# Fifteen small loads between two bulk loads of a row-maximum kernel

## The chip, the cores and the metric

The kernel runs on one core of a Trainium2 chip. The metric is the device time of one execution in microseconds (us). The core's engines that matter here are VectorE (DVE in the profile), which reduces, SyncE (SP), which issues the DMAs that load the input, and the core's 16 DMA engines, which move the bytes.

## The reference

```python
def setup_inputs():
    rows = 8192
    cols = 8192
    return {"x": np.random.randn(rows, cols).astype(np.float32)}

def reference(x):
    return np.linalg.norm(x, ord=np.inf, axis=1)
```

With an axis given, the infinity norm is that of each row as a vector: the largest absolute value of each of the 8192 rows. The input has 268 MB, the output 32 KB.

## The kernel before

The rows are split into two parts. The first 48 rows of each of the 128 partitions are the bulk, the last 16 the tail.

**The bulk.** Two loops, over `a` (six rounds) and `n` (four steps), issue 24 loads from SP (L263). Each brings two rows of 8192 floats to each partition: a tile of 128 x 16384 floats, 8 MB. The tiles lie in `ring`, which has three slots, used in turn. Behind each load stands one reduction on VectorE (L251, in the helper `absmax`), which writes two maxima per partition into `r_bulk`. From the fourth load on, a load has to wait until the reduction three places earlier has freed its slot.

**The tail.** The last 16 rows of each partition come in 30 loads (L296) of decreasing width, from 13056 floats down to 640, listed in `TAIL`. They lie in the same ring. The reductions of the tail write partial maxima into gaps of the ring, and in the end one maximum per row into `r_tail`. Two stores end the kernel: `r_bulk` from ScalarE's queue (L314), three pieces before the end, and `r_tail` from SP (L316).

**What orders the work.** Every engine works through its own list in order; a DMA waits on its issuing engine, here SP, so what is behind it in SP's list waits too. The framework gives each DMA one of eight completion counters in turn (`DMAHW0` to `DMAHW7`, lanes in what follows), and has a DMA wait until the last one on the same lane has landed. [...] The function `drop_implied_waits` strikes out such a wait where SP's wait for VectorE already implies it: a reduction that is over had waited for its load. In SP's list of the kernel before, the 24 bulk loads have no wait for a lane left, only the wait for the reduction that frees their slot; from the fifteenth load of the tail on, the loads have waits for lanes as well, some of them beside a wait for VectorE. Three further functions move the first load to the head of SP's list, let the Pool engine finish the program, and take VectorE out of the opening barrier.

`ring` has 3 x 16384 + 128 floats per partition and is the last tile that is taken from the pool.

Of the kernel before, what the change touches and what calls it, by code (L numbers as in the profile page):

```python
# [12 lines left out]
F32 = mybir.dt.float32  # L13
# [195 lines left out]
@with_exitstack  # L209
def kernel(  # L210
    ctx: ExitStack,
    tc: tile.TileContext,
    x: bass.AP,
    out: bass.AP,
    G: int = 4,
    B: int = 2,
    SLOTS: int = 3,
    PAD: int = 128,
):
    nc = tc.nc  # L220
    P = nc.NUM_PARTITIONS
    rows, cols = x.shape
    W = B * cols
    R = SLOTS * W + PAD * 4


    n_tail = sum(w for _, w in TAIL) // cols
    met = 0
    for lo, w in sorted(TAIL):
        assert lo == met  # L230
        met += w
    assert met == n_tail * cols
    n_bulk_rows = rows // P - n_tail
    assert n_bulk_rows % (G * B) == 0
    A = n_bulk_rows // (G * B)
    split = n_bulk_rows * P
    x_b = x[:split].rearrange("(a p n b) c -> a n p (b c)", p=P, a=A, n=G, b=B)
    out_b = out[:split].rearrange("(a p n b) -> p a (n b)", p=P, a=A, n=G, b=B)
    x_t = x[split:].rearrange("(p t) c -> p (t c)", p=P)
    out_t = out[split:].rearrange("(p t) -> p t", p=P)  # L240

    pool = ctx.enter_context(tc.tile_pool(name="sbuf", bufs=1))
    r_bulk = pool.tile([P, A, G * B], F32)
    r_tail = pool.tile([P, n_tail], F32)
    used = [HEAD, A * G * B, n_tail]
    gap = -sum(-(-n // STEP) * STEP for n in used) % PAD
    pool.tile([P, gap], F32, name="gap")
    ring = pool.tile([P, R], F32)

    def absmax(o, i):  # L250
        return nc.vector.reduce_max(  # L251
            out=o, in_=i, axis=X, apply_absolute_value=True
        )

    def after(ins, first, kind):
        info = mybir.DependencyInfo(kind, mybir.DependencyReason.SCHED_ONLY)
        tc.add_manual_dep(ins.ins, first.ins.name, info, reason="order")

    for a in range(A):
        for n in range(G):  # L260
            at = (a * G + n) % SLOTS * W
            t = ring[:, at : at + W]
            nc.sync.dma_start(out=t, in_=x_b[a, n])  # L263
            absmax(
                r_bulk[:, a, n * B : (n + 1) * B],
                t.rearrange("p (b c) -> p b c", b=B),
            )


    pieces = []  # L270
    for j, (at, w) in enumerate(TAIL):
        end = at + w
        while at < end:
            r = at // cols
            to = min(end, (r + 1) * cols)
            pieces.append((j, r, to - at))
            at = to
    of_row = [[k for k, s in enumerate(pieces) if s[1] == r] for r in range(n_tail)]


    here = A * G % SLOTS * W
    start, slot = [], []
    for j, (_, w) in enumerate(TAIL):
        first = next(s for s in pieces if s[0] == j)
        ks = of_row[first[1]]
        n_part = len(ks) - 1 if pieces[ks[-1]][0] == j else 0
        at = -(-(here + n_part) // PAD) * PAD
        if at + w > R:
            at = -(-n_part // PAD) * PAD
        start.append(at)  # L290
        slot.append(at - n_part)
        here = at + w

    for j, (src, w) in enumerate(TAIL):
        at = start[j]
        nc.sync.dma_start(out=ring[:, at : at + w], in_=x_t[:, src : src + w])  # L296
        here = [k for k, s in enumerate(pieces) if s[0] == j]
        offs = [at + sum(pieces[i][2] for i in here[:m]) for m in range(len(here))]
        todo = list(zip(here, offs))
        if slot[j] != at:  # L300

            todo = todo[1:] + todo[:1]
        for k, lo in todo:
            _, r, n = pieces[k]
            ks = of_row[r]
            if k == ks[-1]:
                frm = slot[j] if len(ks) > 1 else lo
                done = absmax(r_tail[:, r : r + 1], ring[:, frm : lo + n])
            else:
                to = slot[pieces[ks[-1]][0]] + ks.index(k)  # L310
                done = absmax(ring[:, to : to + 1], ring[:, lo : lo + n])
        if j == len(TAIL) - 3:

            ins = nc.scalar.dma_start(out=out_b, in_=r_bulk[:])  # L314
            after(ins, done, mybir.DependencyClass.Sync)
    nc.sync.dma_start(out=out_t, in_=r_tail[:])  # L316
    nc.at_finalize(drop_implied_waits)
    nc.at_finalize(start_first_load_early)
    nc.at_finalize(finish_on_pool)
    nc.at_finalize(open_without_vector)  # L320
# [30 lines left out]
```

## Time and profile before

| What | Value |
|---|---|
| Median of 2 runs | 626.54 us (626.53 to 626.56) |
| The profiled execution's own time | 626.59 us |
| Its span, first to last instruction | 624.0 us |
| VectorE busy | 552.5 us, 66 reductions |
| Read from HBM | 268.44 MB, 430 GB/s over the span with what is written |
| One bulk reduction | 17.22 us |
| VectorE idle before the bulk reductions | 70.5 us in all, the longest 22.0 us |
| SP waiting for VectorE ahead of bulk loads | 417.1 us in 21 waits |
| A bulk load, issue to landing, median | 40.7 us |

A profile's span is shorter than the time of the execution by what lies before its first and behind its last instruction. In the tables of waits, the engine that waits stands on the left, and what ended its wait on the right; "SPq" is SP's list of DMAs. A DMA "lands" when its counter has its last count. The time from issue to landing includes the time in which the DMA lies in the queue behind earlier ones.

### The profile page before, as it was taken

To read this page: it belongs to the slowest core of one execution; us is meant where nothing else is said; L and a number is where in the kernel's file an instruction comes from. 1 tells how busy PE (TensorE), PEld (TensorE's weight loads), DVE (VectorE), ACT (ScalarE), POOL (GpSimd) and SP (SyncE) were. 2 spreads that over 40 slices of the span, in tenths; PEclk is the share of its full clock that TensorE was granted. 3 is DMA by queue.
4 is the path that set the end of the run, shared out by engine and by line. 5 is a ranking of instruction groups with operands and counts; after the bars stand their busy time and mean duration, and the time that the engine had idled before them with its cause. 6 is when DMAs were issued, how large, how long until landed. Compare 5 with 4: busy or idle time off the path is not lost.

```text
span 624.0 us, 153 instructions
## 1 busy us (share of the span) xinstructions
DVE 552.5 (89%) x66; POOL 0.2 (0%) x4
## 2 busy tenths in 40 slices
DVE  0588988889988899888898888988889999999999
POOL 0000000000000000000000000000000000000000
DMA  9999999999999999999999999999999999999998
GB/s 403 458 416 450 424 441 433 403 471 403 471 403 458 416 454 420 450 424 420 454 403 471 403 466 408 458 416 454 420 436 432 417 446 420 428 433 429 429 426 345
DMA packets 8561, 268.47 MB, mean 430 GB/s; under 512 B 1648, under 2 KB 1648, under 8 KB 3184
## 3 DMA queue, kind: packets, MB, share of 16 engines
q1 hardware_dynamic: 7776, 268.44, 99.6%
q10 hardware_dynamic: 784, 0.02, 0.1%
q14 instruction: 1, 0.01, 0.0%
HBM read 268.44 MB, written 0.03 MB: 430 GB/s over the span
## 4 chain that ended last, share of the span: by engine, by line
DMA 64%; DVE 35%; another core or an unknown queue 0%; issue 0%; DVEq 0%; SPq 0%
DMA ring<-in_x_dram 64%; DVE r_bulk L251 25%; DVE r_tail L251 7%; DVE ring L251 3%; DVEq L346 0%; SPq L296 0%
## 5 line engine op out<-in xcount | busy, mean ns | idle before, releaser
L251 DVE TENSOR_REDUCE r_bulk<-ring 128x2 f32<-128x16384 f32 x24 | 413.3, 17220 | 70.5 <-DMA ring<-in_x_dram 70.5
L251 DVE TENSOR_REDUCE ring<-ring 128x1 f32<-128x4736 f32 (+20 forms) x26 | 70.5, 2759 | 0.2 <-DMA ring<-in_x_dram 0.2
L251 DVE TENSOR_REDUCE r_tail<-ring 128x1 f32<-128x8192 f32 (+12 forms) x16 | 70.5, 4428 | 0.0
L335 POOL MEMSET const-bfloat16-1.0<- 128x1 bf16 x1 | 0.1, 103 | 0.0
L335 POOL MEMSET const-uint8-127<- 128x1 uint8 x1 | 0.1, 102 | 0.0
L335 POOL MEMSET const-float32-1.0<- 128x1 f32 x1 | 0.1, 100 | 0.0
L335 POOL MEMSET const-float32-0.0<- 128x1 f32 x1 | 0.1, 99 | 0.2 <-issue 0.2
## 6 DMA issues: line engine op xcount, KB each, us to landing
ring<-in_x_dram SPq DMA_DIRECT2D x1, 6528.0 KB, 32.7
ring<-in_x_dram SPq DMA_DIRECT2D x1, 6464.0 KB, 36.6
ring<-in_x_dram SPq DMA_DIRECT2D x1, 5824.0 KB, 27.1
ring<-in_x_dram SPq DMA_DIRECT2D x1, 5184.0 KB, 39.0
ring<-in_x_dram SPq DMA_DIRECT2D x1, 4672.0 KB, 36.8
ring<-in_x_dram SPq DMA_DIRECT2D x1, 4096.0 KB, 32.7
ring<-in_x_dram SPq DMA_DIRECT2D x1, 3648.0 KB, 40.9
ring<-in_x_dram SPq DMA_DIRECT2D x1, 3264.0 KB, 36.8
```

Source lines behind the costliest of these rows:

```text
L251: return nc.vector.reduce_max(out=o, in_=i, axis=X, apply_absolute_value=True)
L335: nc = _bacc.Bacc("TRN2", target_bir_lowering=False, num_devices=1)
```

## The change

A further tile `marks` of 16 partitions x 256 floats is taken from the pool behind `ring`. When the loop over the bulk has issued the load of `a == 2`, `n == 1`, the tenth of the 24, SP issues fifteen further loads, for k = 1 to 15. The k-th reads 16 floats (64 bytes) from each of the first k rows of the same block of the input and writes them to k partitions of `marks`, each to columns of its own. Nothing reads `marks`. The eleventh bulk load follows.

```diff
@@ -246,6 +246,7 @@
     gap = -sum(-(-n // STEP) * STEP for n in used) % PAD
     pool.tile([P, gap], F32, name="gap")
     ring = pool.tile([P, R], F32)
+    marks = pool.tile([16, 256], F32)
 
     def absmax(o, i):
         return nc.vector.reduce_max(
@@ -261,6 +262,12 @@
             at = (a * G + n) % SLOTS * W
             t = ring[:, at : at + W]
             nc.sync.dma_start(out=t, in_=x_b[a, n])
+            if a == 2 and n == 1:
+                for k in range(1, 16):
+                    nc.sync.dma_start(
+                        out=marks[:k, 16 * k : 16 * k + 16],
+                        in_=x_b[a, n][:k, 16 * k : 16 * k + 16],
+                    )
             absmax(
                 r_bulk[:, a, n * B : (n + 1) * B],
                 t.rearrange("p (b c) -> p b c", b=B),
```

In SP's list of the changed program the fifteen loads take the lanes 2 to 7, 0 to 7 and 0. The first five have no wait. The sixth to the fifteenth each wait for the lane that they take, and so do the eight bulk loads that follow them, these beside their wait for VectorE. The list of VectorE is the same.

## The prediction

> I number the 24 bulk loads 0 to 23 in the order in which they are issued. The fifteen small loads stand behind load 9 (a = 2, n = 1) and ahead of load 10; I call them s1 to s15 by their partition count.
>
> **What bounds the kernel now.** I read the page first: the two rows of busy tenths, the chain that ended last and the costliest group.
>
> ```profile
> span 624.0 us, 153 instructions
> ...
> DVE 552.5 (89%) x66; POOL 0.2 (0%) x4
> ...
> DMA  9999999999999999999999999999999999999998
> ...
> DMA ring<-in_x_dram 64%; DVE r_bulk L251 25%; DVE r_tail L251 7%; DVE ring L251 3%; DVEq L346 0%; SPq L296 0%
> ...
> L251 DVE TENSOR_REDUCE r_bulk<-ring 128x2 f32<-128x16384 f32 x24 | 413.3, 17220 | 70.5 <-DMA ring<-in_x_dram 70.5
> ```
>
> The DMA row is at 9 in every slice but the last. VectorE is 89% busy, but it idles before each bulk reduction, and what it waits for is the load. So the load stream is the bound, from the first microsecond to the end: a gap in it is paid in full unless later work can catch it up. The chain names VectorE for 35%, yet VectorE and the transfers only alternate there; the stream never stops under it.
>
> Next the timeline around load 9, VectorE and SP's queue in turn:
>
> ```profile
> 22.04 17.22 DVE L251 TENSOR_REDUCE r_bulk<-ring 128x2 f32<-128x16384 f32 x1 [22.04 <-DMA ring<-in_x_dram]
> 41.34 17.22 DVE L251 TENSOR_REDUCE r_bulk<-ring 128x2 f32<-128x16384 f32 x1 [2.08 <-DMA ring<-in_x_dram]
> ...
> 155.27 0.33 SPq L263 DMA_DIRECT2D ring<-in_x_dram  x1
> 157.42 17.22 DVE L251 TENSOR_REDUCE r_bulk<-ring 128x2 f32<-128x16384 f32 x1 [2.18 <-DMA ring<-in_x_dram]
> 174.67 0.33 SPq L263 DMA_DIRECT2D ring<-in_x_dram  x1
> 176.74 17.22 DVE L251 TENSOR_REDUCE r_bulk<-ring 128x2 f32<-128x16384 f32 x1 [2.10 <-DMA ring<-in_x_dram]
> ...
> 196.03 17.22 DVE L251 TENSOR_REDUCE r_bulk<-ring 128x2 f32<-128x16384 f32 x1 [2.07 <-DMA ring<-in_x_dram]
> ...
> 215.34 17.22 DVE L251 TENSOR_REDUCE r_bulk<-ring 128x2 f32<-128x16384 f32 x1 [2.09 <-DMA ring<-in_x_dram]
> ```
>
> The bulk reductions follow each other by load, so the one at 22.04 is load 0's, at 41.34 load 1's, at 157.42 load 7's, at 176.74 load 8's, at 196.03 load 9's and at 215.34 load 10's. A reduction starts 0.02 us after its load has landed. The step from one landing to the next is 19.3 us, and a load that starts into an idle queue (load 0, issued at 0.00) needs 22.02 us: 2.7 us more than its share of a running stream. SP issues load 9 at 155.27 (the end of load 6's reduction, which frees its slot) and load 10 at 174.67 (the end of load 7's). While load 9 is being moved, load 10 has thus been in the queue for 21 us. Nothing else stands in the queue behind load 9 before 174.67.
>
> Last, what SP waits for, what one of its issues takes, and the shortest DMA there is:
>
> ```profile
> SPq L263 <- DVE r_bulk L251: 417.1, 21, 37.5
> ...
> SPq L296 <- DMA ring<-in_x_dram: 54.0, 15, 6.6
> ```
>
> ```profile
> L263 SPq DMA_DIRECT2D ring<-in_x_dram x24: 327/328/638, 0.0 to 425.8; - x24
> ...
> DMA to landing us min/median/max: 22.0/40.7/59.5
> ```
>
> ```profile
> 0.77 0.33 SPq L263 DMA_DIRECT2D ring<-in_x_dram  x1
> ...
> 1.15 0.64 SPq L263 DMA_DIRECT2D ring<-in_x_dram  x1
> ```
>
> ```profile
> out_dram<-r_tail SPq DMA_DIRECT2D x1, 8.0 KB, 1.4
> ```
>
> In the bulk part SP waits for VectorE only. In the tail (L296) it also waits for earlier loads: DMAs take eight counters (lanes) in turn, and a DMA has to wait for the one eight places ahead of it, unless another wait has already told SP that that one has landed. For the bulk loads the wait for VectorE tells just that.
>
> **The change, part by part.** It removes nothing, and VectorE's list is the same. SP gets fifteen DMAs between load 9 and load 10.
>
> *Bytes.* 120 rows of 64 bytes are 7.7 KB beside 268 MB. At 8 MB per 19.3 us that is 0.02 us. I cost it at nothing.
>
> *Issue time alone.* Fifteen issues of about 0.4 us are 6 us. Between 155.60 and 174.67 SP only waits, so this would be hidden, with 13 us to spare. If that were all, the change would cost nothing.
>
> *The waits.* Loads 0 to 9 took lanes 0 to 7, 0 and 1. So s1 to s5 take lanes 2 to 6, whose loads 2 to 6 are known to have landed: no wait. In SP's order in the changed program s6 waits for lane 7, that is load 7; s7 for lane 0, load 8; s8 for lane 1, load 9. Then s9 to s15 wait for s1 to s7, and load 10 for s8 and for VectorE. Loads 11 to 17 wait for s9 to s15 in the same way. SP works in order, so load 10 stands behind all of it. With the times of before:
> - load 7 lands at 157.40, about when s5 has been issued (155.27 + 6 x 0.4 = 157.7): no wait worth a number.
> - load 8 lands at 176.72; s7 goes then. Load 10 was issued at 174.67 before, so it is late from here on.
> - load 9 lands at 196.01 and s8 goes at 196.03. Nothing is left in the queue now: load 9 was the last large one. The stream is dry.
> - s9 to s15 wait for s1 to s7, which lie in the queue right behind load 9; they have landed or do so within the next microsecond. I cost these waits at nothing; covered by the issues ahead of each. Load 10's own wait for s8: issued at 196.03, landing 1.4 us later by the row of r_tail, 197.4, covered by the seven issues s9 to s15.
>
> *From s8 to load 10.* Eight issues, s8 to s15, one behind the other, then load 10. The step between issues: 0.33 us (an issue's own length) is the low end, 0.64 (the third load in a row at the start) the high end. The start shows 0.38 from the second issue to the third (0.77 to 1.15). I take 0.40, near this row, a little above it since the third was slower: 8 x 0.40 = 3.2 us. Load 10 is issued at 199.2.
>
> [...]
>
> *Load 10 into the idle queue.* 22.02 us, as load 0: it lands at 221.2 instead of 215.32, 5.9 us late. The ends: with 0.33 a step, and half a microsecond off because load 0 may have paid for a cold start, 4.9; with 0.64 a step 7.8, and with something more for the engines' fewer counts some 9.4 (0.84 a step, 0.2 more).
>
> *What is late next.* Load 11, which waits for load 8's reduction (over at 193.96) and for s9, goes right behind load 10, so the stream is full again with two loads in the queue. Load 12 goes at 213.3 as before (load 9's reduction is not moved), load 13 behind load 10's reduction, 19 us ahead of its need. From there everything is shifted by the same amount. VectorE idles 5.9 us more once, ahead of load 10's reduction, and its 2.1 us of idle time per load can't catch anything up: the stream sets the pace. In the tail the waits eight places back are the same ones as before. There is no slack at the end either; the queue is full until 621.
>
> The sum is made against the profiled execution: span 624.0 us, time 626.59, so 2.6 us lie around the span; it stands 0.05 us above the median of 626.54. 626.59 + 5.9 = 632.5 us, 0.9% slower.
>
> **The rivals.**
>
> *Hidden: no change, 626.6 us.* If load 10 is issued by 193.3 (its landing at 215.32 less 22.02), the queue never runs dry. That decides: nothing ahead of load 10 may wait for load 9. It would be so with more lanes, or with six small loads; then the last large landing that holds SP up is load 8's at 176.72, and with all eight issues behind it 176.7 + 8 x 0.4 = 179.9. For it speaks that the bulk part of before waits for no load at all (417.1 us, all for VectorE). Against it stands the order of the changed program, in which s8 and load 9 share a lane.
>
> *One after the other.* If the small loads don't overlap (each issued only when the one before has landed), the eight from s8 on take 8 x 1.8 us (0.4 of issue and 1.4 of landing) = 14.4 instead of 3.2, and the time is 643.7. For it speaks only how short each of them is beside its landing; against it that each waits for one eight places back. [...]
>
> *Slow small issues.* If an issue on 1 to 15 partitions takes some 1 us, 8 us stand in place of 3.2: 637.3, 1.7% slower. No row is like it; the 0.64 us is the longest.
>
> *Faster.* It would need a stream that runs quicker after a stop. After the start from rest the first steps are 19.30 and 19.33 us, as all later ones: nothing for it.
>
> **How the numbers follow.** The forecast with its ends (631.5 to 636.0) gets 0.84, hidden 0.05, slow small issues 0.05, one after the other 0.05, faster 0.01. The range 630.8 to 636.2 is the forecast's ends with a little room (other cold-start costs on load 0); the others, 16 in 100, lie outside. Over 2%, 12.5 us, is about what a measurement of this kernel can tell from no change: slower by that only in the serial case and a part of the slow issues, 0.06; faster by that 0.01; within 2%, 0.93.
>
> **What would show it right or wrong.** Right: one idle gap of VectorE of about 8 us (2.1 + 5.9) ahead of load 10's reduction, all others at 2.1; SP waiting for a load's landing ahead of two of the small loads, s7 and s8, about 19 us each; load 10 issued near 199.2, landing 22 us later; one slice of DMA and GB/s that dips near 200 us; the reductions before 196 unmoved and all after 221 late by one amount. Wrong: load 10 issued before 193 (hidden); several gaps of the stream, or gaps between s8 and s15 (one after the other); small issues longer than 0.45 us; or a shift at 221 that the later loads do not keep.

## The result, and the profile after

The changed kernel takes 632.28 us (632.26 and 632.30) against 626.54: 5.74 us more, a ratio of 1.009 (95% interval 1.0073 to 1.0106). The forecast was 632.5.

The page of the changed kernel, the parts that were read before:

```profile
span 629.6 us, 176 instructions
...
DVE 552.5 (88%) x66; POOL 0.2 (0%) x4
...
DMA  9999999999996999999999999999999999999998
GB/s 400 466 400 466 400 466 400 466 400 466 400 466 267 450 416 450 416 454 412 454 412 462 404 466 400 466 400 466 400 452 421 440 437 429 432 422 434 425 425 348
...
L252 DVE TENSOR_REDUCE r_bulk<-ring 128x2 f32<-128x16384 f32 x24 | 413.3, 17220 | 76.3 <-DMA ring<-in_x_dram 76.3
```

The span is 5.6 us longer and VectorE's busy time the same. In the DMA row one slice, the thirteenth (189 to 205 us), has fallen from 9 to 6, and its rate to 267 GB/s; all others look like before. VectorE's idle time before the bulk reductions is up from 70.5 to 76.3 us. So there is one gap, and it sits where the small loads are. The same in stretches of 5 us (length, VectorE's busy time and count, Pool's, TensorE's clock, share of the DMA engines, GB/s):

```profile
195.00:200.00 5.00, 4.05 (x1) 0.00 (x0) 1.00 0.03 2
200.00:205.00 5.00, 5.00 (x1) 0.00 (x0) 1.00 1.09 419
```

Between 195 and 200 us the DMA engines move next to nothing. The timeline around it (start, length, engine, line, and idle time before it in brackets):

```profile
155.22 0.33 SPq L264 DMA_DIRECT2D ring<-in_x_dram  x1
155.59 2.01 SPq L267 DMA_DIRECT2D marks<-in_x_dram  x6
...
176.65 0.27 SPq L267 DMA_DIRECT2D marks<-in_x_dram  x1
176.66 17.22 DVE L252 TENSOR_REDUCE r_bulk<-ring 128x2 f32<-128x16384 f32 x1 [2.09 <-DMA ring<-in_x_dram]
...
195.94 2.97 SPq L267 DMA_DIRECT2D marks<-in_x_dram  x8
195.94 17.22 DVE L252 TENSOR_REDUCE r_bulk<-ring 128x2 f32<-128x16384 f32 x1 [2.07 <-DMA ring<-in_x_dram]
199.02 0.83 SPq L264 DMA_DIRECT2D ring<-in_x_dram  x2
...
220.93 17.22 DVE L252 TENSOR_REDUCE r_bulk<-ring 128x2 f32<-128x16384 f32 x1 [7.76 <-DMA ring<-in_x_dram]
240.32 17.22 DVE L252 TENSOR_REDUCE r_bulk<-ring 128x2 f32<-128x16384 f32 x1 [2.18 <-DMA ring<-in_x_dram]
```

Read it by SP's lines. Load 9 and s1 to s6 go between 155.22 and 157.60; s7 goes alone when load 8 has landed (176.65); s8 to s15 go in a row when load 9 has landed (195.94); and only at 199.02 do loads 10 and 11 follow. VectorE then idles 7.76 us ahead of load 10's reduction, and 2.18 ahead of the next one, as ever. What SP waited for ahead of the small loads:

```profile
SPq L267 <- DMA ring<-in_x_dram: 38.2, 3, 19.0
```

38.2 us in three waits, the longest 19.0: two of about 19 us, for loads 8 and 9, and one of next to nothing.

### The profile page after: what moved, and what is told of

The parts are those of the page before. It is cut to its first block, busy times and chain, and to the rows that moved or that the text cites. A ratio compares the mean times of both kernels' runs of the same rounds, so it can differ in the third digit from the quotient of the medians.

```text
span 629.6 us, 176 instructions
## 1 busy us (share of the span) xinstructions
DVE 552.5 (88%) x66; POOL 0.2 (0%) x4
## 4 chain that ended last, share of the span: by engine, by line
DMA 67%; DVE 32%; SPq 1%; issue 0%; DVEq 0%
DMA ring<-in_x_dram 67%; DVE r_bulk L252 22%; DVE r_tail L252 7%; DVE ring L252 3%; SPq L267 0%; DVEq L353 0%; SPq L264 0%; SPq L303 0%
## 5 line engine op out<-in xcount | busy, mean ns | idle before, releaser
L252 DVE TENSOR_REDUCE r_bulk<-ring 128x2 f32<-128x16384 f32 x24 | 413.3, 17220 | 76.3 <-DMA ring<-in_x_dram 76.3
L252 DVE TENSOR_REDUCE ring<-ring 128x1 f32<-128x4736 f32 (+20 forms) x26 | 70.5, 2761 | 0.1
```

The lines of the kernel that those rows point to most:

```text
L252: return nc.vector.reduce_max(out=o, in_=i, axis=X, apply_absolute_value=True)
```

## The experiments

Theory 1 is the prediction's: SP works in order, a small load takes the lane of a bulk load that is still in flight, so SP stands until that has landed, and the next bulk load is issued only when the queue is dry. The price is then that of a restart plus the issues that stand between the landing and the next bulk load, and it hangs on where the small loads stand and how many go in a row. Theory 2, the rival: each small load costs the stream something, by its issue or by its short packets. By it the price hangs on their number alone. All kernels are edits of the changed one; the times are compared with the kernel before in the same series (626.57 to 626.68 us).

**six: where the stop should not occur**

```diff
-                for k in range(1, 16):
+                for k in range(1, 7):
```

> Only the first six small loads (1 to 6 partitions) are issued behind load 9. Theory 1 (a small load takes the lane of load 9, so SP stands until load 9 has landed, and the stream runs dry): load 10 then takes the lane of load 8, which lands at 176.7; it is issued near 176.8, 19 us before load 9 lands, nothing runs dry: 626.5 to 626.8 us, no idle time of VectorE above 2.3 us after the first load. Load 11 waits for load 9 (195.9 instead of 194.0), which is hidden too. Theory 2 (each small load costs the stream something, by its issue or by its short packets): 6/15 of the 5.7 us, 628.8 us.

626.74 us, ratio 1.0001 (0.9991 to 1.001). The reduction of load 10 has no idle time ahead of it beyond the usual:

```profile
215.56 17.22 DVE L252 TENSOR_REDUCE r_bulk<-ring 128x2 f32<-128x16384 f32 x1 [2.09 <-DMA ring<-in_x_dram]
```

Six small loads cost nothing that can be measured; theory 2 asked for 2.3 us.

**seven: one more**

```diff
-                for k in range(1, 16):
+                for k in range(1, 8):
```

> One more than six (1 to 7 partitions). Theory 1: load 10 itself takes the lane of load 9 and is issued when load 9 has landed, near 196.0, with no small load between: it lands 21.9 us later, at 217.9 instead of 215.3. 2.6 us more than before, 629.2 us. This is the price of the dry queue alone. Theory 2 (a cost per small load): 7/15 of 5.7 us, 629.2 us as well, but only 0.4 us above the kernel with six; theory 1 has a step of 2.5 us between six and seven.

629.82 us, ratio 1.0049 (1.0034 to 1.0064): a step of 3.1 us between six and seven.

```profile
195.90 17.22 DVE L252 TENSOR_REDUCE r_bulk<-ring 128x2 f32<-128x16384 f32 x1 [2.06 <-DMA ring<-in_x_dram]
195.96 17.52 SPq L264 DMA_DIRECT2D ring<-in_x_dram  x3
217.91 17.22 DVE L252 TENSOR_REDUCE r_bulk<-ring 128x2 f32<-128x16384 f32 x1 [4.79 <-DMA ring<-in_x_dram]
```

Load 10 is issued at 195.96, the moment load 9 has landed, with no small load between, and VectorE's wait grows from 2.06 to 4.79 us. 2.7 us is the price of the dry queue alone. The median lies 0.6 us above the expected 629.2, the profiled execution (629.21) on it; that difference, and the rest of the 3.1 us, are within the spread of the kernel before in this series (626.37 to 627.51).

**spread: all fifteen, one at a time**

```diff
-            if a == 2 and n == 1:
-                for k in range(1, 16):
-                    nc.sync.dma_start(
+            k = a * G + n - 4
+            if 1 <= k < 16:
+                nc.sync.dma_start(
...
```

> All fifteen small loads (1 to 15 partitions), but one behind each of the loads 5 to 19 instead of all behind load 9. Theory 1: each waits for the DMA eight places back, four bulk loads earlier, which has long landed; nothing stands: 626.5 to 626.9 us. Theory 2 (a cost per small load, wherever it stands): 632.3 us.

626.71 us, ratio 1.0003 (0.9994 to 1.0013). The same fifteen DMAs on the same queue cost nothing when they don't stand in one place. This is where theory 2 falls.

**sixteen: even partition counts**

```diff
-                        out=marks[:k, 16 * k : 16 * k + 16],
-                        in_=x_b[a, n][:k, 16 * k : 16 * k + 16],
+                        out=marks[:16, 16 * k : 16 * k + 16],
+                        in_=x_b[a, n][:16, 16 * k : 16 * k + 16],
```

> The fifteen small loads stand where the change puts them, but each has 16 partitions. Theory 1: the same waits, so the same stop at load 9's landing; only the eight issues from s8 on can differ: between 0.30 us each (if what makes them longer is the uneven partition count) and 0.43 us (if they go on growing with the partitions, 0.38 long at 15). 631.6 to 632.7 us. A rival (the uneven counts upset the DMA engines' shares, 1 to 15 of 16 in use): with 16 partitions that is gone, 626.6 to 629.

633.44 us, ratio 1.0108 (1.0093 to 1.0123), 0.7 us above the expected range; the rival of the uneven counts is out. The timeline of this kernel, and its small loads' lengths (minimum, median, maximum in ns) ahead of those of the changed kernel:

```profile
196.16 3.55 SPq L267 DMA_DIRECT2D marks<-in_x_dram  x8
...
199.82 13.92 SPq L264 DMA_DIRECT2D ring<-in_x_dram  x3
221.79 17.22 DVE L252 TENSOR_REDUCE r_bulk<-ring 128x2 f32<-128x16384 f32 x1 [8.40 <-DMA ring<-in_x_dram]
```

```profile
L267 SPq DMA_DIRECT2D marks<-in_x_dram x15: 311/418/438, 155.7 to 199.3; - x15
```

```profile
L267 SPq DMA_DIRECT2D marks<-in_x_dram x15: 236/296/382, 155.6 to 198.5; - x15
```

The eight issues take 3.66 us (196.16 to 199.82), 0.46 a step instead of the 0.385 of the changed kernel: issues of 16 partitions are longer, not shorter. The gap follows: 8.40 - 2.09 = 6.3 us. The range allowed 0.43 a step, which accounts for 0.2 us of the miss; the other 0.5 us stays open (the kernel before spread from 626.37 to 627.51 in this series).

**pool and act: other queues**

```diff
-                    nc.sync.dma_start(
+                    nc.gpsimd.dma_start(      # pool; nc.scalar.dma_start in act
```

> The fifteen small loads are issued from GpSimd's queue instead of SP's. They take lanes of that queue's own, SP's list is that of the kernel before, and they run early, since they wait for nothing of SP's. Theory 1: no stop, 626.5 to 627.0 us. Theory 2 (a cost per small load): up to 632.3 us.

> The fifteen small loads are issued from ScalarE's queue, in the lanes that SP's loads use as well. Since ScalarE has nothing else to wait for, they run at the start; loads 1 to 8 on SP then wait for lanes that small loads had. Theory 1: what counts is whether a bulk load's issue is put off past the landing of the load ahead of it. Load 1 waits for a small load that should land within some 3 us, load 0 at 22: no stop, 626.5 to 627.0 us. If the small loads of the second queue stood behind load 0 in the DMA engines, loads 1 and 2 would go at 22 us instead of 1: 2.6 us more, 629.2 us.

pool: 627.06 us, ratio 1.0004 (0.9994 to 1.0014), no stop; the median is 0.06 us above its range. act: 629.69 us, ratio 1.0048 (1.0033 to 1.0063): 0.5 us above the second branch of its expectation (the profiled execution took 629.15), and not the first. In act, the timeline at the start and SP's waits:

```profile
21.98 17.22 DVE L252 TENSOR_REDUCE r_bulk<-ring 128x2 f32<-128x16384 f32 x1 [21.98 <-DMA ring<-in_x_dram]
44.17 17.22 DVE L252 TENSOR_REDUCE r_bulk<-ring 128x2 f32<-128x16384 f32 x1 [4.98 <-DMA ring<-in_x_dram]
```

```profile
SPq L264 <- DMA marks<-in_x_dram: 27.8, 3, 21.4
```

SP waited 21.4 us for a small load before it could issue load 1, about as long as load 0 took. By the counters in the trace this was s8: issued at 9.10 us, when s1 had landed and so freed the lane, and landed at 22.12; load 1 went at 22.14. The gap is of the same kind and size as in seven (4.98 - 2.1 = 2.9 us), at another place, and made by waits for small loads instead of bulk loads. In pool the small loads landed as late as this, but none of SP's DMAs shares a lane with them (issue to landing, us: minimum, median, maximum):

```profile
DMA to landing us min/median/max: 8.6/33.6/36.5
```

One more rival would put a step between six and seven: that SP's queue holds only eight DMAs at a time, whatever the lanes. act speaks against it, since SP stops there with a single load of its own in flight. A kernel with the small loads in place and their waits struck out was not run.

**thirty: twice the number**

```diff
-    marks = pool.tile([16, 256], F32)
+    marks = pool.tile([16, 512], F32)
...
-                for k in range(1, 16):
+                for k in range(1, 31):
...
-                        out=marks[:k, 16 * k : 16 * k + 16],
-                        in_=x_b[a, n][:k, 16 * k : 16 * k + 16],
+                        out=marks[: k % 15 + 1, 16 * k : 16 * k + 16],
+                        in_=x_b[a, n][: k % 15 + 1, 16 * k : 16 * k + 16],
```

> Thirty small loads (2 to 15, 1 to 15 and 1 partitions) at the place of the change instead of fifteen. Theory 1: one stop at the same place; the issues between load 9's landing and load 10 grow from 8 to 23. The issues of the changed kernel stepped by 0.28 (2 partitions) to 0.43 us (15), 0.35 in the mean: 15 x 0.35 = 5.3 us more than the change, 637.5 us (636.5 to 638.5). A rival (the stop is the cost, the issues are hidden): 632.3 us. Another rival (the stop comes again for each eight): 632.3 plus two more stops of 2.6, and the issues, over 640 us.

637.73 us, ratio 1.0175 (1.016 to 1.0191), inside the range.

```profile
196.05 8.17 SPq L267 DMA_DIRECT2D marks<-in_x_dram  x23
...
204.34 39.52 SPq L264 DMA_DIRECT2D ring<-in_x_dram  x4
226.29 17.22 DVE L252 TENSOR_REDUCE r_bulk<-ring 128x2 f32<-128x16384 f32 x1 [13.01 <-DMA ring<-in_x_dram]
```

23 issues in a row, 8.29 us from the first to load 10, 0.36 a step; VectorE idles 13.01 us ahead of load 10's reduction, once. The stop comes once; the issues behind it add up.

**by_six and by_seven: the same fifteen in bunches**

```diff
-            if a == 2 and n == 1:
-                for k in range(1, 16):
+            bunch = {9: (1, 7), 10: (7, 13), 11: (13, 16)}    # by_seven: (1, 8), (8, 15), (15, 16)
+            if a * G + n in bunch:
+                for k in range(*bunch[a * G + n]):
```

> All fifteen small loads, in three bunches: 1 to 6 partitions behind load 9, 7 to 12 behind load 10, 13 to 15 behind load 11. Theory 1 (what costs time is a bulk load put off past the landing of the one ahead of it): load 10 waits for load 8 (176.7) and goes 19 us early; the first of the second bunch waits for load 9 (196.0) and load 11 goes near 198, 17 us before load 10 lands; the first of the third waits for load 10 (215.3), and load 12 goes near 216.5, 18 us before load 11 lands. No gap in the stream: 626.5 to 626.9 us. Theory 2 (a cost per small load): 632.3.

> The same fifteen, with seven in a bunch: 1 to 7 behind load 9, 8 to 14 behind load 10, 15 behind load 11. Theory 1: load 10 takes the lane of load 9 and load 11 that of load 10, so the stream runs dry twice, and no small load is issued in either gap: two gaps of 2.6 us in place of none, VectorE idle 4.8 us ahead of the reductions of load 10 and of load 11: 626.6 + 5.3 = 631.9 us (631.4 to 632.4). If only one gap can occur (the second load in a row being in the queue in time), 629.2.

by_six: 626.97 us, ratio 1.0006 (0.9996 to 1.0015), 0.07 us above its range and without a gap. by_seven: 632.58 us, ratio 1.0091 (1.0076 to 1.0106). The two gaps of by_seven in its timeline:

```profile
196.95 2.74 SPq L268 DMA_DIRECT2D marks<-in_x_dram  x7
218.54 17.22 DVE L252 TENSOR_REDUCE r_bulk<-ring 128x2 f32<-128x16384 f32 x1 [4.82 <-DMA ring<-in_x_dram]
...
240.58 17.22 DVE L252 TENSOR_REDUCE r_bulk<-ring 128x2 f32<-128x16384 f32 x1 [4.82 <-DMA ring<-in_x_dram]
259.97 17.22 DVE L252 TENSOR_REDUCE r_bulk<-ring 128x2 f32<-128x16384 f32 x1 [2.17 <-DMA ring<-in_x_dram]
```

Twice 4.82, then 2.17 again: two gaps of 2.7 us. The seven small loads at 196.95 are issued behind load 10 (196.55), while it is being moved, and cost nothing there; load 11 behind them has to wait for load 10, which is the second gap. The time is 0.2 us above the range; load 9's reduction starts at 196.50 in this profile, 0.6 us later than in seven, ahead of any gap. Moving one small load per bunch thus turns a cost of 0.9% into none. by_six keeps the change's fifteen loads within three bulk loads at no measurable cost; no run beats the kernel before.

## Why the prediction was right, step by step

- *What bounds the kernel.* The load stream does: VectorE's busy time did not change, and every gap of the stream, in all kernels with one, went to the end of the run: the spans grew by 2.6 us in seven, 5.6 in the changed kernel and 11.1 in thirty.
- *The bytes and the issue time cost nothing by themselves.* For the bytes spread, pool and by_six show it, for SP's issue time spread and by_six.
- *The waits.* s6 went without a wait worth a number, s7 at load 8's landing, s8 at load 9's. Predicted for s8: 196.03; measured: 195.94.
- *s9 to s15 and load 10 don't wait beyond the issues ahead of them.* The eight issues run one behind the other up to load 10. By the counters in the trace s1 to s7 landed between 195.48 and 196.57, each ahead of the issue that waits for it (s9 at 196.25 to s15 at 198.53), and s8 at 197.18, 1.2 us after its issue where the prediction had 1.4. The rival "one after the other" (643.7 us) is out.
- *The eight issues.* Predicted 3.2 us; measured 195.94 to 199.02, 3.08, or 0.385 a step. That the mean lies so near the 0.40 is in part luck: the prediction took it from issues on 128 partitions, while these eight got longer with the partition count, from 0.27 to 0.38 us, and on 16 partitions the steps were 0.46 (sixteen).
- *Load 10 into the idle queue.* Predicted 22.02 us to landing; measured 220.91 - 199.02 = 21.9.
- *The shift.* Predicted 5.9 us ahead of load 10's reduction; measured 7.76 - 2.09 = 5.7. Both small terms were 0.1 us too high, and that is the 0.2 us between 632.5 and 632.28.
- *What is late next.* Loads 10 and 11 went back to back, the next wait of VectorE was 2.18, and nothing was caught up.

The two terms were also taken apart by experiments. What VectorE idles beyond its usual 2.09 us, less the time from the first of the issues to load 10:

| Kernel | Issues in the gap | Their time | Gap | Rest |
|---|---|---|---|---|
| seven | 0 | 0 | 2.70 | 2.7 |
| changed | 8 | 3.08 | 5.67 | 2.6 |
| sixteen | 8 | 3.66 | 6.31 | 2.7 |
| thirty | 23 | 8.29 | 10.92 | 2.6 |

The rest is one number within 0.1 us, whatever the small loads: the 2.7 us by which load 0 was longer than its share of a running stream. So load 0 paid for nothing at the start of the program that a restart does not pay too, and the half microsecond that the low end took off for a cold start was not there.

One term at the upper end of the range, the "engines' fewer counts" (0.84 us a step, and 0.2 us more), no run shows. In its place the runs showed steps of 0.385 us in the mean, and behind a pause, when nothing else is being issued, s7 took 0.27 us (176.65 in the timeline), the shortest of the 16-partition loads 0.31 and the bulk load of 128 partitions 0.33. Of the eight issues from s8 to s15 the one on the fewest partitions was the shortest, 0.27 us, and each after it longer, up to 0.38.

What stays open: the issues in a row get longer with the partition count, from 0.24 us (two partitions) to 0.38 (15) and 0.42 (16); s1, on one partition and right behind a bulk load, breaks the row with 0.34. The runs give the numbers, not the cause. What the 2.7 us of a restart consist of was not taken apart either.

## What to carry to other kernels

A DMA that is small and unused can still stop a queue: count how many DMAs back its completion counter was last used, and whether that one is still in flight. Here six DMAs between two bulk loads were free and the seventh cost 2.7 us, because the eighth place back is then the load that is just being moved. If small DMAs must share a queue with a stream, keep at most six between two large loads (by_six, 626.97 us), spread them out (spread, 626.71), or give them a queue with counters of its own (pool, 627.06); and once the queue is dry, each further issue ahead of the next large load adds its full time, 0.36 to 0.46 us in the mean here.

## What the runs showed of the hardware that was not expected

A tiny load was not quick beside a full stream here, even from another queue: from GpSimd's queue loads of 64 to 960 bytes took 8.6 to 36.5 us from issue to landing (part of it behind each other), and in act SP stood 21.4 us for one from ScalarE's queue, where the expectation had some 3 us. In the trace of act a record of a bulk load's 64 KB row lasts 2.42 us (median of the 3072), and while load 0 is being moved the records of ScalarE's queue come in six short groups, which start at 6.26, 8.61, 11.06, 13.48, 15.90 and 18.36 us, with none between them: steps of 2.35 to 2.46 us, each about as long as one row's record. The issues of pool have like steps:

```profile
15.01 0.51 POOL L267 DMA_DIRECT2D marks<-in_x_dram  x1 [4.33 <-DMA marks<-in_x_dram]
19.86 0.50 POOL L267 DMA_DIRECT2D marks<-in_x_dram  x1 [4.34 <-DMA marks<-in_x_dram]
22.46 0.50 POOL L267 DMA_DIRECT2D marks<-in_x_dram  x1 [2.10 <-DMA marks<-in_x_dram]
```

These lines are the timeline of pool; the bracket is the time GpSimd waited for an earlier small load to land before it issued the next. The first two are 4.85 us apart, about two of the 2.42 us records; the last two 2.60 us, about one. That the rows being moved are the cause of the slow landings is an estimate from these times; no experiment changed the length of a row to test it.
